# Gate and up of 18 of 22 column pairs by seven products of quarters

## The chip, the cores and the metric

The kernel runs on one core of one Trainium2 chip. The metric is device time in microseconds (us) of one execution; runs of the same program lie within some tenths of a per cent of each other. A core has five engines that work side by side and wait for each other by semaphores: TensorE (PE, matmuls, with its weight loads shown as PEld), VectorE (DVE), ScalarE (ACT), GpSimd (POOL) and SyncE (SP, which here only issues DMA transfers).

## The reference

A decoder trunk of two layers on 512 tokens of width 1024, all in float32. A layer has three attention mixers on one input projection, cross-attention into 256 memory tokens, and a SwiGLU FFN of inner width 2816. What matters here is the FFN:

```
h = rmsnorm(x, norm_ffn[l])
gate_h, up_h = jnp.split(h @ w_gate_up[l], 2, axis=-1)
x = x + (jax.nn.silu(gate_h) * up_h) @ w_down[l]
```

Float32 precision is kept by splitting every operand into a high part (a float32r cast, by ACT) and a low part (the rest, a subtraction on DVE) and by adding three matmuls: high x high, high x low, low x high.

## The kernel before

Activations lie with features on the 128 partitions and the 512 tokens along the row, in eight tiles of 128 features. A weight unit is 128 output columns for all 1024 inputs: a tile of 128 x 1024. `proj` takes one unit: `mm3` (L230) issues 3 matmuls of 512 tokens for each of 8 blocks, 24 in all, into one of three PSUM banks `mm`.

Units are used in a fixed order, the plan. `unit` and `ahead` (L175, L194) load three units on (`load`, SP, three buffers `wraw`) and split one unit on (`halve`: cast `wh` on ACT at L222, subtraction `wl` on DVE at L163; two buffers each). In the FFN the whole `wl` is DVE's (`vcols` is 8).

`skew` (L67) staggers tasks: a task's work after its matmuls is issued behind the matmuls of the next task. Tile, the layer beneath, may then move an instruction on its engine where its operands allow it.

`ffn` (L1190) has 22 pairs of units, gate j and up j. `gate` multiplies its result by 1/rms (`rstd`) as it leaves PSUM and applies Silu; `up` does the same multiplication, multiplies by the gate and splits the product into `h`. The rows of h fall into three parts of 8, 8 and 6; after each part eight `down` tasks add h @ w_down to x. In the last layer the third part's down runs in two halves of 256 tokens (`down_half`, L1238), with the weights kept in `kh` and `kl`. The operand of gate and up is x times the gain, split in `xh` and `xl` before the rms is known, which is why 1/rms is applied afterwards.

## Time and profile before

| what | value |
|---|---|
| median of 3 runs | 2079.9 us (2078.93 to 2082.0) |
| the profiled execution: time, span in the profile | 2081.03 us, 2079.3 us |
| PE, DVE, ACT, POOL busy | 2025.2, 1235.1, 1087.0, 346.4 us |
| Silu of the gates, first layer | 681.8 to 1002.9 us of the span |
| Silu of the gates, second layer | 1705.0 to 2027.1 us |

A time on a row of the profile is an instruction's own duration. Instructions of one engine overlap at their ends, above all matmuls, so that the distance from start to start is what each one costs its engine. "[2.40 <-PE mm L239]" says that the engine was idle for 2.40 us before this instruction and what ended it. The granted clock of TensorE is 1.00 at its upper level of 2.4 GHz and 0.50 at 1.2 GHz.

### The profile page before, as it was taken

How to read it: one execution, taken by the hardware profiler on the slowest of the kernel's cores; microseconds unless marked ns; L12 is line 12 of the kernel's file. 1: busy time of each engine (PE TensorE's matmuls, PEld its weight loads, DVE VectorE, ACT ScalarE, POOL GpSimd, SP SyncE). 2: the span in 40 equal slices, each digit the busy share in tenths (PEclk: the TensorE clock that was granted, in tenths of full speed). 3: DMA queues.
4: the chain of work that ended last, by engine and by line, in shares of the span. 5: the costliest groups of instructions: out<-in, count | busy, mean ns of one | idle time of the engine just before them, and what ended most of it. 6: DMA issues, size and time to landing. Idle time of an engine off the chain costs nothing. (4 is left out here: it accounts for less than half of the span.)

```text
span 2079.3 us, 27775 instructions
## 1 busy us (share of the span) xinstructions
PE 2025.2 (97%) x10072; PEld 1658.0 (80%) x10072; DVE 1235.1 (59%) x2462; ACT 1087.0 (52%) x2196; POOL 346.4 (17%) x302
## 2 busy tenths in 40 slices
PE   7999999999999999999999999999999999999998
PEld 5878887878887788888877788878788878888887
DVE  7786777665457443434567867676655664444354
ACT  5676786884456322222456767777744652222232
POOL 4332122222212000000133212232122010000000
PEclk9999999999999999999999999999999999999999
DMA  6321212233332222322343122132333323233331
GB/s 188 103 73 57 67 46 87 79 105 105 109 102 74 89 92 92 101 91 92 127 123 106 57 67 66 54 88 73 109 117 95 108 68 95 91 92 93 99 107 56
DMA packets 66145, 189.49 MB, mean 91 GB/s; under 512 B 10056, under 2 KB 15944, under 8 KB 66008
## 3 DMA queue, kind: packets, MB, share of 16 engines
q1 hardware_dynamic: 66008, 187.72, 29.3%
q8 instruction: 79, 1.29, 0.3%
q14 instruction: 58, 0.48, 0.1%
HBM read 171.92 MB, written 4.75 MB: 85 GB/s over the span
## 5 line engine op out<-in xcount | busy, mean ns | idle before, releaser
L222 ACT CAST wh<-wraw 128x1024 fp32r<-128x1024 f32 (+3 forms) x311 | 315.4, 1014 | 643.9 <-PE mm L238 364.4
L237 PE MATMUL mm<-xh,wh 128*128 128x512 f32 x1504 | 612.2, 407 | 7.7 <-ACT wh L222 6.3
L238 PE MATMUL mm<-xl,wh 128*128 128x512 f32 x1504 | 602.2, 401 | 2.6 <-DVE xl L173 2.6
L239 PE MATMUL mm<-xh,wl 128*128 128x512 f32 x1504 | 602.6, 401 | 2.0 <-DVE wl L163 1.7
L163 DVE TENSOR_TENSOR wl<-wraw,wh 128x1024 fp32r<-128x1024 f32 (+6 forms) x311 | 339.0, 1090 | 71.6 <-ACT wh L222 65.0
L239 PEld LDWEIGHTS mm<-xh,wl 128*128 128x128 f32 x1504 | 285.5, 190 | 69.1 <-DVE wl L163 3.7
L237 PEld LDWEIGHTS mm<-xh,wh 128*128 128x128 f32 x1504 | 285.9, 190 | 68.0 <-ACT wh L222 6.3
L238 PEld LDWEIGHTS mm<-xl,wh 128*128 128x128 f32 x1504 | 285.9, 190 | 65.5 <-DVE xl L173 5.5
L163 DVE TENSOR_TENSOR tmp<-mm,rstd 128x512 f32<-128x512 f32 (+1 forms) x138 | 90.9, 659 | 275.4 <-PE mm L239 255.6
L163 POOL TENSOR_TENSOR wl<-wraw,wh 128x512 fp32r<-128x512 f32 (+4 forms) x112 | 161.6, 1444 | 518.4 <-ACT wh L222 416.0
L518 ACT ACTIVATE p<-p,st 128x256 f32<-128x256 f32 (+5 forms) x288 | 155.3, 539 | 42.8 <-DVE st L512 38.7
L163 POOL TENSOR_TENSOR acc<-acc,tmp 128x512 f32<-128x512 f32 (+1 forms) x55 | 74.2, 1349 | 599.6 <-ACT tmp L265 438.4
L163 DVE TENSOR_TENSOR x<-x,mm 128x512 f32<-128x512 f32 (+1 forms) x88 | 55.6, 638 | 182.0 <-PE mm L239 182.0
L170 DVE TENSOR_TENSOR pl<-tp,ph 128x256 fp32r<-128x256 f32 (+3 forms) x288 | 131.1, 457 | 50.1 <-ACT ph L169 48.7
L530 ACT ACTIVATE p<-p,st 128x256 f32<-128x256 f32 (+3 forms) x288 | 142.4, 532 | 28.9 <-DVE st L163 17.5
L169 ACT CAST ph<-tp 128x256 fp32r<-128x256 f32 (+3 forms) x288 | 113.1, 395 | 41.1 <-PE tp L448 38.7
L448 PE MATMUL tp<-ident,p 128*128 128x128 f32 x656 | 122.3, 278 | 9.6 <-DVE pl L170 3.6
L512 DVE CUSTOM_DVE_ANT_0 p<-s,causal 128x128 f32<-128x128 f32 (+2 forms) x224 | 106.4, 477 | 41.0 <-PE s L917 16.7
L238 PE MATMUL mm<-h,wh 128*128 128x512 f32 x304 | 120.2, 396 | 0.0
L239 PE MATMUL mm<-h,wl 128*128 128x512 f32 x304 | 120.2, 396 | 0.0
L237 PE MATMUL mm<-h,wh 128*128 128x512 f32 x304 | 120.1, 395 | 0.0
L448 PEld LDWEIGHTS tp<-ident,p 128*128 128x128 f32 x656 | 78.4, 140 | 31.5 <-DVE pl L170 8.7
(242 smaller groups left out, 3297.9 us busy)
## 6 DMA issues: line engine op xcount, KB each, us to landing
wraw<-in_w_in SPq DMA_DIRECT2D x91, 512.0 KB, 3.6
wraw<-in_w_gu SPq DMA_DIRECT2D x88, 512.0 KB, 3.5
wraw<-in_w_d SPq DMA_DIRECT2D x32, 512.0 KB, 3.4
wraw<-in_w_br SPq DMA_DIRECT2D x24, 512.0 KB, 3.6
wraw<-in_w_xkv SPq DMA_DIRECT2D x16, 512.0 KB, 3.4
wraw<-in_w_out SPq DMA_DIRECT2D x16, 512.0 KB, 3.5
wraw<-in_w_d SPq DMA_DIRECT2D x16, 384.0 KB, 3.2
wraw<-in_w_xq SPq DMA_DIRECT2D x8, 512.0 KB, 3.4
```

What stands on the lines that cost most here:

```text
L163: (eng or self.nc.vector).tensor_tensor(out=out, in0=a, in1=b, op=op)
L169: nc.scalar.copy(hi, src)
L170: (eng or nc.vector).tensor_tensor(out=lo, in0=src, in1=hi.bitcast(F32), op=OP.subtract)
L222: nc.scalar.copy(wh[:, j:j + n], raw[:, j:j + n])
L237: nc.tensor.matmul(ps, wh[:, c], xh, start=i == 0, stop=False)
L238: nc.tensor.matmul(ps, wh[:, c], xl, start=False, stop=False)
L239: nc.tensor.matmul(ps, wl[:, c], xh, start=False, stop=i == len(blocks) - 1)
L448: self.nc.tensor.transpose(tp[:, j], src[:, j * 128:j * 128 + 128], self.ident)
L512: o.nc.vector.tensor_tensor_reduce(out=p, in0=self.ps.pop(i), in1=self.mask(self.blocks[i]), scale=-self.scale, scalar=self.init, op0=OP.a ...
L518: self.o.nc.scalar.activation(p, p, AF.Exp, scale=-1.0, bias=st[:, 0, i:i + 1], accum_out=st[:, 1, i:i + 1])
L530: nc.scalar.activation(self.p[j], self.p[j], AF.Copy, scale=self.st[:, 2, j:j + 1])
```

## The change

Four pairs of each layer (j = 0 to 3) stay as they were, apart from a sign. For the other 18 the four quarters of a pair's weights (gate and up, first and second half of the 1024 inputs) and the four quarters of the operand (halves of the inputs, halves of the tokens) are multiplied in the Strassen-Winograd way: seven products p1 to p7 of 128 x 512 by 512 x 256. Each product is `quads`: four blocks of three matmuls of 256 tokens.

- Weight sums: unit `S31` holds gate + up of the first input half and up first + up second half; unit `S24` two further sums built on it; `A22` is the second half of up. Sums and low parts are made on DVE, casts on ACT. The raw up weights have a tile of their own, `up`, with two buffers, read by the sums of S31 and last by the low part of A22 (`dl`). S24 and A22 have one buffer, S31 two.
- Operand: `normed` multiplies x by gain and 1/rms, `sums` makes four differences T (two on GpSimd, two on DVE) and splits them, `operand` writes the split normalised x over the old `xh`, `xl` while the last plain `up` runs through its blocks.
- Results: p1, p6, p7 and p4 of a pair are added up in one PSUM bank (A), and what stands there is copied out in between (s1, s2 by ACT, U by DVE); p5 and p3 share a second bank (D); p2 has a third. Gate halves go to G, up halves to U, with the negative sign that `down` takes off.
- Order: p1(j), p7(j-1), p5(j), p2(j), p4(j-1), p6(j), p3(j), so that a pair's last two products stand among the next pair's. The eight `down` of a part come after p3 of pairs 8 and 16.

```diff
+SUMS, AHEAD, PLAIN = ("S31", "S24", "A22"), 5, 4
...
-        self.load(i + 3)
+        self.load(self.reach(i))
         self.halve(i)
...
+    def reach(self, i):
+
+        plain, j = 0, i
+        while j + 1 < len(self.plan) and j < i + AHEAD and plain < 3:
+            j += 1
+            plain += self.plan[j][0][0] not in SUMS
+        return j
...
     def ahead(self):
         if self.plan is not None:
-            self.load(self.used + 3)
-            self.halve(self.used)
+            i = self.used
+            self.load(self.reach(i))
+            near = [u[0][0] for u in self.plan[i:i + 3]]
+            self.halve(i + 2 if any(t in SUMS for t in near) else i)
...
+            if src[0] in SUMS:
+                self.raw[self.loaded] = self.load_sum(*src)
+                self.loaded += 1
+                continue
...
+            if self.plan[i][0][0] in SUMS:
+                self.ready[i] = self.halve_sum(raw, *self.plan[i][0])
+                self.halved += 1
+                continue
+            if self.plan[i][0][0] == "w_gu":
+                self.gate_raw = raw
...
+    def load_sum(self, kind, l, j):
+
+        if kind != "S31":
+            return None
+        up = self.ups[j] = self.ff.tile([128, 1024], F32, name="up", tag="up", bufs=2)
+        self.nc.sync.dma_start(up, self.a["w_gu"][l, 2 * j + 1])
+        return up
+
+    def halve_sum(self, raw, kind, l, j):
+
+        nc, ff, gate = self.nc, self.ff, self.gate_raw
+        if kind == "A22":
+            h, lo = (ff.tile([128, 512], F32R, name="d" + t, tag="d" + t, bufs=1) for t in "hl")
+            self.split(h, lo, self.ups.pop(j)[:, 512:])
+            return h, lo
+        k = 2 if kind == "S31" else 1
+        s = ff.tile([128, 1024], F32, name="sum", tag=kind + "r", bufs=k)
+        h, lo = (ff.tile([128, 1024], F32R, name=kind + t, tag=kind + t, bufs=k) for t in "hl")
+        if kind == "S31":
+            self.tt(s[:, :512], gate[:, :512], raw[:, :512], OP.add)
+            self.tt(s[:, 512:], raw[:, :512], raw[:, 512:], OP.add)
+            self.sum_raw = s
+        else:
+            self.tt(s[:, :512], self.sum_raw[:, 512:], gate[:, :512], OP.add)
+            self.tt(s[:, 512:], s[:, :512], gate[:, 512:], OP.add)
+        self.split(h, lo, s)
+        return h, lo
...
+    def quads(self, ps, w, off, x, start=True, ahead=False):
+
+        nc = self.nc
+        wh, wl = w
+        for i, (xh, xl) in enumerate(x):
+            c = slice(off + i * 128, off + i * 128 + 128)
+            for k, (a, b) in enumerate(((wh, xh), (wh, xl), (wl, xh))):
+                nc.tensor.matmul(ps, a[:, c], b, start=start and i + k == 0, stop=i == 3 and k == 2,
+                                 skip_group_check=not start)
+            if ahead and i == 0:
+                self.ahead()
+            yield 354
...
+        def up(j):
+            w = self.unit("w_gu", l, 2 * j + 1)
+            ps = self.mm()
+            for i, c in enumerate(self.mm3(ps, w, range(KT), x, ahead=1)):
+                yield c
+                if j == PLAIN - 1 and i % 4 == 3:
+                    operand(range(i - 3, i + 1))
...
+        def normed(kk):
...
+            y = ff.tile([128, 2, 512], F32, name="y", tag="h", bufs=9)
+            for j in range(2):
+                k = 2 * kk + j
+                c = l * G_LAYER + G_FFN + k
+                nc.vector.scalar_tensor_tensor(y[:, j], xt[k], self.gains[:, c:c + 1], n["r"], op0=OP.mult, op1=OP.mult)
+            ys[kk] = y
+
+        def sums(i):
+
+            if i == 0:
+                ts.extend([[ff.tile([128, 4, 256], F32R, name="T", tag="T", bufs=8) for _ in "hl"] for _ in range(4)])
+            c, f = slice(2 * i, 2 * i + 2), [self.tmp((128, 2, 256)) for _ in range(4)]
+            b11, b12, b21, b22 = (ys[k][:, :, h] for k in (i, 2 + i) for h in (slice(0, 256), slice(256, 512)))
+            self.tt(f[0], b11, b12, OP.subtract, nc.gpsimd)
+            self.tt(f[2], b22, b12, OP.subtract, nc.gpsimd)
+            nc.vector.scalar_tensor_tensor(f[1], f[0], -1.0, b22, op0=OP.mult, op1=OP.subtract)
+            nc.vector.scalar_tensor_tensor(f[3], f[1], -1.0, b21, op0=OP.mult, op1=OP.subtract)
+            for t, src in zip(ts, f):
+                self.split(t[0][:, c], t[1][:, c], src)
+
+        def operand(ks):
+
+            for k in ks:
+                c = slice(0, 256 if k < 4 else 512)
+                self.split(x[k][0][:, c], x[k][1][:, c], ys[k // 2][:, k % 2, c])
...
+        def gated(s, c, ps, other):
+            g = s.get("G")
+            if g is None:
+                s["G"] = self.tmp()
+            self.tt(s["G"][:, c], ps, other, OP.add)
+            if g is not None:
+                nc.scalar.activation(g, g, AF.Silu)
+
+        def p1(j):
+            s = pairs[j] = {"A": bank("s", 2)}
+            s["w"] = self.unit("w_gu", l, 2 * j)
+            yield from self.quads(s["A"], s["w"], 0, part_of(0, 0), ahead=True)
+            yield STAGE
+            s["s1"] = kept(s["A"], "s1")
+
+        def p2(j):
+            s = pairs[j]
+            ps = bank("av", 1)
+            yield from self.quads(ps, s["w"], 512, part_of(1, 0))
+            yield STAGE
+            gated(s, slice(0, 256), ps, s["s1"])
+
+        def p5(j):
+            s = pairs[j]
+            s["w31"] = self.unit("S31", l, j)
+            s["D"] = bank("tp", 2)
+            yield from self.quads(s["D"], s["w31"], 512, trans(0), ahead=True)
+            yield STAGE
+            s["s5"] = kept(s["D"], "s5")
+
+        def p6(j):
+            s = pairs[j]
+            s["w24"] = self.unit("S24", l, j)
+            yield from self.quads(s["A"], s["w24"], 0, trans(1), False, ahead=True)
+            yield STAGE
+            s["s2"] = kept(s["A"], "s2")
+
+        def p3(j):
+            s = pairs[j]
+            yield from self.quads(s["D"], s["w24"], 512, part_of(1, 1), False)
+            yield STAGE
+            gated(s, slice(256, 512), s["D"], s["s2"])
+
+        def p7(j):
+            s = pairs[j]
+            yield from self.quads(s["A"], s["w31"], 0, trans(2), False)
+            yield STAGE
+            s["U"] = self.tmp()
+            self.tt(s["U"][:, 256:], s["A"], s["s5"], OP.add)
+
+        def p4(j):
+            s = pairs[j]
+            w = self.unit("A22", l, j, nblk=4)
+            yield from self.quads(s["A"], w, 0, trans(3), False, ahead=True)
+            yield STAGE
+            u, g = s["U"], s["G"]
+            self.tt(u[:, 256:], u[:, 256:], g[:, 256:], OP.mult)
+            self.tt(u[:, :256], s["A"], g[:, :256], OP.mult)
+            o = ff.tile([128, 2, 512], F32R, name="h", tag="h", bufs=9)
+            self.split(o[:, 0], o[:, 1], u)
+            hs[min(j // 8, 2)].append((o[:, 0], o[:, 1]))
+            del pairs[j]
+
+        def after(task, *calls):
+            yield from task
+            for f, i in calls:
+                f(i)
...
-            self.tt(xt[i], xt[i], ps, OP.add)
+            self.tt(xt[i], xt[i], ps, OP.subtract)
...
+        m = sum(FFN_PARTS) - 1
+        tasks = [self.norm_end(st, D, n), gate(0), up(0), after(gate(1), (normed, 0), (normed, 2)),
+                 after(up(1), (normed, 1), (normed, 3)), after(gate(2), (sums, 0)), after(up(2), (sums, 1))]
+        tasks += [gate(3), up(3)]
+        for j in range(PLAIN, m):
+            old = [p7(j - 1), p4(j - 1)] if j > PLAIN else [None, None]
+            new = [p1(j), old[0], p5(j), p2(j), old[1], p6(j), p3(j)]
+            tasks += [t for t in new if t is not None]
+            if j in (8, 16):
+                tasks += [down(i, j // 8 - 1) for i in range(KT)]
+        tasks += [p1(m), p7(m - 1), p5(m), p6(m), p4(m - 1), p3(m), p7(m), p2(m), p4(m)]
```

Not shown: the tiles that hold the last layer's kept weights, the final outputs and the accumulators of the norm take over buffers of the new tiles, `down_half` subtracts too, and four short helpers pick slices.

In the rows below a name's number tells its buffer use; "waits" names the engines or DMA queues whose semaphores an instruction waits for.

First VectorE in the middle of the first layer's FFN, two projections of the kernel before: the gate's and up's results come from bank `mm`, each with the next unit's low part.

```order
L163 TENSOR_TENSOR tmp_8166<-mm_8101,rstd_7062 128x512 [waits PE_49]
L163 TENSOR_TENSOR tmp_8166<-tmp_8166,tmp_8132 128x512 [waits DVE_49,Activation_49]
L163 TENSOR_TENSOR wl_8145<-wraw_8037,wh_8144 128x1024 [waits DMAHW0_49,Activation_49]
L170 TENSOR_TENSOR h_8169<-tmp_8166,h_8169 128x512 [waits Activation_49]
L163 TENSOR_TENSOR tmp_8203<-mm_8135,rstd_7062 128x512 [waits PE_49]
L163 TENSOR_TENSOR wl_8182<-wraw_8071,wh_8181 128x1024 [waits DMAHW1_49,Activation_49]
```

The same place now, one steady pair but for its last two instructions (G's right half, `tp + s2`, and the low part of S24): sums of S31 and S24 (`sum`), U (`s + s5`), G's left half (`av + s1`), low parts `S31l`, `wl`, `dl`.

```order
L166 TENSOR_TENSOR sum_8470<-wraw_8338,up_8361 128x512 [waits DMAHW0_49]
L166 TENSOR_TENSOR sum_8470<-up_8361 128x512
L166 TENSOR_TENSOR tmp_8448<-s_8266,s5_8333 128x256 [waits PE_49]
L166 TENSOR_TENSOR sum_8529<-sum_8470,wraw_8338 128x512 [waits DVE_49]
L166 TENSOR_TENSOR tmp_8448<-tmp_8448,tmp_8356 128x256 [waits DVE_49,Activation_49]
L173 TENSOR_TENSOR S31l_8472<-sum_8470,S31h_8471 128x1024 [waits Activation_49]
L166 TENSOR_TENSOR sum_8529<-sum_8529,wraw_8338 128x512 [waits DVE_49]
L166 TENSOR_TENSOR tmp_8486<-av_8450,s1_8429 128x256 [waits PE_49]
L166 TENSOR_TENSOR wl_8566<-wraw_8468,wh_8565 128x1024 [waits DMAHW6_49,Activation_49]
L173 TENSOR_TENSOR dl_8494<-up_8241,dh_8493 128x512 [waits PE_49,Activation_49]
L166 TENSOR_TENSOR tmp_8448<-s_8266,tmp_8356 128x256
L173 TENSOR_TENSOR h_8508<-tmp_8448,h_8508 128x512 [waits Activation_49]
```

What moved: two results and two low parts per pair became fourteen instructions. The last read of bank `s` (`tmp_8448<-s_8266`) stands behind `wl` and `dl`, and `h` behind it.

SyncE's loads in the first layer's FFN, before:

```order
L205 DMA wraw_7284<-in_w_gu 128x1024 [waits DMAHW7_49,DVE_49]
L205 DMA wraw_7318<-in_w_gu 128x1024 [waits DMAHW0_49,DVE_49]
L205 DMA wraw_7355<-in_w_gu 128x1024 [waits DMAHW1_49,DVE_49]
L205 DMA wraw_7389<-in_w_gu 128x1024 [waits DMAHW2_49,DVE_49]
L205 DMA wraw_7426<-in_w_gu 128x1024 [waits DMAHW3_49,DVE_49]
```

And now, in the steady part (gate units go to `wraw`, up units to `up`):

```order
L222 DMA wraw_8728<-in_w_gu 128x1024 [waits DMAHW5_49,DVE_49]
L260 DMA up_8491<-in_w_gu 128x1024 [waits DVE_49]
L222 DMA wraw_8858<-in_w_gu 128x1024 [waits DMAHW6_49,DVE_49]
L260 DMA up_8621<-in_w_gu 128x1024 [waits DMAHW0_49,DVE_49]
L222 DMA wraw_8988<-in_w_gu 128x1024 [waits DMAHW7_49,DVE_49]
L260 DMA up_8751<-in_w_gu 128x1024 [waits DMAHW2_49,DVE_49]
```

What moved: gate and up loads still alternate, but each kind has its own buffers, and an up load waits for DVE's last read of the up tile before the last.

VectorE at the first pair of seven products of layer 0, from the last sum of the operand's splits on; in the kernel before this place has the rows of the first excerpt.

```order
L166 TENSOR_TENSOR sum_7349<-sum_7295,wraw_7182 128x512
L173 TENSOR_TENSOR xl0_6857<-y_7169,xh0_6856 128x256 [waits PE_49]
L166 TENSOR_TENSOR sum_7349<-sum_7349,wraw_7182 128x512 [waits DVE_49]
L173 TENSOR_TENSOR xl1_6877<-y_7169,xh1_6876 128x256 [waits PE_49]
L173 TENSOR_TENSOR xl2_6904<-y_7212,xh2_6903 128x256 [waits Activation_49]
L173 TENSOR_TENSOR xl3_6925<-y_7212,xh3_6924 128x256 [waits Activation_49]
L173 TENSOR_TENSOR xl4_6952<-y_7172,xh4_6951 128x512 [waits Activation_49]
L173 TENSOR_TENSOR S24l_7351<-sum_7349,S24h_7350 128x1024 [waits Activation_49]
L173 TENSOR_TENSOR xl5_6973<-y_7172,xh5_6972 128x512 [waits PE_49]
L173 TENSOR_TENSOR xl6_7000<-y_7215,xh6_6999 128x512 [waits PE_49]
L173 TENSOR_TENSOR xl7_7008<-y_7215,xh7_7007 128x512 [waits Activation_49]
L166 TENSOR_TENSOR tmp_7390<-mm_7278,rstd_7062 128x512
```

What moved: the second low part of a weight sum stands between the low parts of x that p1 and p2 read, and the result of the last plain gate (`mm_7278`) comes behind them.

## Rows read from the trace of the kernel before

**Rows 1.** The page, busy time and the clock in 40 slices.
```profile
PE 2025.2 (97%) x10072; PEld 1658.0 (80%) x10072; DVE 1235.1 (59%) x2462; ACT 1087.0 (52%) x2196; POOL 346.4 (17%) x302
...
PEclk9999999999999999999999999999999999999999
```
**Rows 2.** Stretches: start:end, length, busy us (instructions) by engine, clock, DMA share, GB/s.
```profile
100.00:200.00 100.00, 94.28 (x527) 76.05 (x526) 77.47 (x217) 73.25 (x187) 28.87 (x29) 1.00 0.23 69
700.00:800.00 100.00, 100.00 (x429) 80.41 (x428) 40.84 (x48) 25.38 (x31) 0.00 (x0) 1.00 0.30 95
800.00:900.00 100.00, 100.00 (x429) 80.40 (x428) 44.10 (x52) 27.36 (x33) 0.00 (x0) 1.00 0.29 91
...
2032.00:2066.00 34.00, 33.11 (x276) 32.85 (x275) 16.75 (x40) 8.69 (x19) 0.00 (x0) 1.00 0.10 32
```
**Rows 3.** DVE in order of time, one pair: start, duration, engine, line, operation, out<-in.
```profile
833.66 0.69 DVE L163 TENSOR_TENSOR tmp<-mm,rstd 128x512 f32<-128x512 f32 x1 [2.40 <-PE mm L239]
...
839.27 0.69 DVE L163 TENSOR_TENSOR tmp<-mm,rstd 128x512 f32<-128x512 f32 x1 [3.50 <-PE mm L239]
840.07 0.69 DVE L163 TENSOR_TENSOR tmp<-tmp 128x512 f32<-128x512 f32 x1
840.68 1.22 DVE L163 TENSOR_TENSOR wl<-wraw,wh 128x1024 fp32r<-128x1024 f32 x1
841.82 0.68 DVE L170 TENSOR_TENSOR h<-tmp,h 128x512 fp32r<-128x512 f32 x1
844.90 0.69 DVE L163 TENSOR_TENSOR tmp<-mm,rstd 128x512 f32<-128x512 f32 x1 [2.40 <-PE mm L239]
```
**Rows 4.** PE in order of time, first and last of 67 matmuls of `down_half`.
```profile
2059.75 0.28 PE L239 MATMUL mm<-h,kl 128*128 128x256 f32 x1
...
2067.67 0.28 PE L239 MATMUL mm<-h,kl 128*128 128x256 f32 x1
```
**Rows 5.** Groups of ACT, 700 to 1000 us: count, busy, mean ns, idle before.
```profile
L222 ACT CAST wh<-wraw 128x1024 fp32r<-128x1024 f32 x53 | 55.8, 1053 | 208.7 <-PE mm L238 136.1 <-issue 72.7
L1200 ACT ACTIVATE tmp<-tmp 128x512 f32<-128x512 f32 x19 | 11.9, 626 | 0.0
L169 ACT CAST h<-tmp 128x512 fp32r<-128x512 f32 x19 | 11.8, 621 | 12.5 <-DVE tmp L163 12.5
```
**Rows 6.** Groups of the whole span: 256 columns on ACT, a kept weight on DVE.
```profile
L169 ACT CAST xos<-av 128x256 fp32r<-128x256 f32 x16 | 6.0, 374 | 4.6 <-PE av L580 4.6
...
L163 DVE TENSOR_TENSOR kl<-wraw,kh 128x768 fp32r<-128x768 f32 x8 | 7.6, 955 | 3.1 <-ACT kh L222 3.1
```
**Rows 7.** DVE in order of time: 256 columns back to back, and behind a matmul.
```profile
632.55 0.42 DVE L170 TENSOR_TENSOR xos<-av,xos 128x256 fp32r<-128x256 f32 x1
632.89 0.41 DVE L170 TENSOR_TENSOR xv<-tp,xv 128x256 fp32r<-128x256 f32 x1
...
2067.99 0.42 DVE L163 TENSOR_TENSOR x<-x,mm 128x256 f32<-128x256 f32 x1 [0.77 <-PE mm L239]
```
**Rows 8.** SP's issue behind `wl`, and DMA: count, KB, median us to landing.
```profile
841.93 0.33 SPq L205 DMA_DIRECT2D wraw<-in_w_gu  x1
...
wraw<-in_w_gu SPq DMA_DIRECT2D x88, 512.0 KB, 3.5
...
w<-in_nsa_w SPq DMA_DIRECT2D x4, 512.0 KB, 5.2
...
DMA to landing us min/median/max: 2.3/3.5/7.0
```
**Rows 9.** DVE in order of time, before the first FFN.
```profile
652.52 1.41 DVE L173 SCALAR_TENSOR_TENSOR xl<-x,gains,xh 128x512 fp32r<-128x512 f32 x2
...
656.18 3.49 DVE L173 SCALAR_TENSOR_TENSOR xl<-x,gains,xh 128x512 fp32r<-128x512 f32 x2
```
**Rows 10.** POOL in the same stretch.
```profile
656.02 3.10 POOL L163 TENSOR_TENSOR acc<-acc,tmp 128x512 f32<-128x512 f32 x2 [0.93 <-ACT tmp L265]
```

More of the change, by code (lines that the diff above doesn't have):

```diff
@@ L116, in drain @@
         pass
+SUMS, AHEAD, PLAIN = ("S31", "S24", "A22"), 5, 4
+KEEP = [("T", 8)] * 8 + [("S31h", 2)] * 2 + [("S31l", 2)] * 2 + [("S31r", 2)] * 2 + [("S24h", 1), ("S24l", 1)]
 CUTS, W1, POS, SQP = 2, 4, 5, (1, 2, 3, 4)
@@ L213, in halve @@
             raw, n = self.raw.pop(i), self.plan[i][1] * 128
+            if self.plan[i][0][0] in SUMS:
[4 more added lines that the diff above has]
+                self.gate_raw = raw
             if self.plan[i][0] in self.kept:
-                wh, wl = (self.ff.tile([128, n], F32R, name=f"k{t}", tag=f"k{t}", bufs=KT) for t in "hl")
+                k = 2 * self.kept.index(self.plan[i][0])
+                wh, wl = (self.ff.tile([128, 1024], F32R, name="kept", tag=KEEP[k + t][0], bufs=KEEP[k + t][1])
+                          for t in range(2))
             else:
@@ L258, in norm_tile @@
         if st["acc"] is None:
-            sq = st["acc"] = st["pool"].tile([128, n], F32, name="acc", tag="acc", bufs=2 if n == 256 and st["pool"] is not self.sh else 1)
+            tag, bufs = ("acc", 1) if st["pool"] is self.sh else ("s5", 2)
+            sq = st["acc"] = st["pool"].tile([128, n], F32, name="acc", tag=tag, bufs=bufs)
             new = True
@@ L1194, in ffn @@
         gs, hs = {}, [[] for _ in FFN_PARTS]
+        self.ff, self.ups = ff, {}
+        ys, ts, pairs = {}, [], {}
         def gate(j):
@@ L1200, in gate @@
             nc.scalar.activation(g, g, AF.Silu)
-        def up(j, part):
-            ps = yield from self.proj(("w_gu", l, 2 * j + 1), x)
+        def up(j):
[5 more added lines that the diff above has]
+                    operand(range(i - 3, i + 1))
             yield STAGE
             u = self.evac(ps, n["r"])
-            self.tt(u, u, gs.pop(j), OP.mult)
+            nc.vector.scalar_tensor_tensor(u, u, -1.0, gs.pop(j), op0=OP.mult, op1=OP.mult)
@@ L1207, in up @@
             o = ff.tile([128, 2, 512], F32R, name="h", tag="h", bufs=9)
             self.split(o[:, 0], o[:, 1], u)
-            hs[part].append((o[:, 0], o[:, 1]))
+            hs[0].append((o[:, 0], o[:, 1]))
+        def normed(kk):
[5 more added lines that the diff above has]
+            ys[kk] = y
@@ new lines, in operand, with part_of, trans, kept @@
+        def operand(ks):
+            for k in ks:
+                c = slice(0, 256 if k < 4 else 512)
+                self.split(x[k][0][:, c], x[k][1][:, c], ys[k // 2][:, k % 2, c])
+        def part_of(k, h):
+            return [(a[:, h * 256:h * 256 + 256], b[:, h * 256:h * 256 + 256]) for a, b in x[4 * k:4 * k + 4]]
+        def trans(i):
+            return [(ts[i][0][:, b], ts[i][1][:, b]) for b in range(4)]
+        def kept(ps, name):
+            s = ff.tile([128, 256], F32, name=name, tag=name, bufs=2 if name == "s5" else 1)
+            nc.scalar.copy(s, ps)
+            return s
@@ new lines, in bank @@
+        def bank(tag, bufs):
+            return self.ps.tile([128, 512], F32, name=tag, tag=tag, bufs=bufs)[:, :256]
+        def gated(s, c, ps, other):
[11 more added lines that the diff above has]
+            s["s1"] = kept(s["A"], "s1")
@@ L1220, in down @@
                 self.norm_tile(st2, xt[i])
-        tasks, f0 = [self.norm_end(st, D, n)], 0
-        for part, kn in enumerate(FFN_PARTS):
-            new = [t for j in range(f0, f0 + kn) for t in (gate(j), up(j, part))]
-            if part:
-                tasks += new[:1] + [down(i, part - 1) for i in range(KT)] + new[1:]
-            else:
-                tasks += new
-            f0 += kn
+        m = sum(FFN_PARTS) - 1
[9 more added lines that the diff above has]
+        tasks += [p1(m), p7(m - 1), p5(m), p6(m), p4(m - 1), p3(m), p7(m), p2(m), p4(m)]
         if not last:
@@ L1232, in ffn @@
             return st2, n2
-        self.ff, self.kept = ff, [("w_d2", l, i) for i in range(KT)]
+        self.kept = [("w_d2", l, i) for i in range(KT)]
         ws, sh, rh = {}, [self.norm_begin(256, nc.vector, ff) for _ in range(2)], [{}, {}]
@@ L1245, in down_half @@
             yield STAGE
-            self.tt(xt[i][:, c], xt[i][:, c], ps, OP.add)
+            self.tt(xt[i][:, c], xt[i][:, c], ps, OP.subtract)
             if i == 0 and half == 0:
@@ L1253, in final @@
             for i in range(KT):
-                t = ff.tile([128, 256], F32, name="fin", tag="fin", bufs=8)
+                if i % 4 == 0:
+                    f = ff.tile([128, 4, 256], F32, name="fin", tag="up", bufs=2)
+                t = f[:, i % 4]
                 c, g = slice(256 * half, 256 * half + 256), G_FINAL + i
```

## The prediction

> **What bounds the kernel now.** I read the busy times of the page first, then the stretches of the two FFNs, then one pair of projections on VectorE, then the only place with the instruction that the change multiplies. On the page TensorE (PE) is busy 97% of the span at a clock of 9 tenths or more in every slice [rows 1]. In the FFN stretches PE shows no idle time at all, VectorE (DVE) is busy 41 to 44% and ScalarE (ACT) 25 to 27% [rows 2]. So there the time is the number of matmuls times their spacing. The busy durations (0.39 us) overlap and are no spacing; the spacing is read from DVE, which takes the result of one 24-matmul projection at 833.66, of the next at 839.27 and of a third at 844.90 [rows 3]: 11.24 us for two, so 11.24 / 48 = 0.234 us per matmul of 512 columns. The pace of 256 columns is seen where the last down projection runs in halves: one starts at 2059.75, and 66 starts later one at 2067.67 [rows 4], 7.92 / 66 = 0.120 us, with the weight loads under them.
>
> **What goes and what comes on PE.** A pair (gate and up) was 48 matmuls, 11.24 us. It becomes seven products of 4 blocks by 3 matmuls of 256 columns, 84 x 0.120 = 10.08 us. That is 1.16 us per pair, and 36 pairs in two layers give 41.8 us. This is all that the change can bring, and only if nothing else makes PE wait. Bounds on the 0.120: it is taken where DVE and ACT are at most half busy [rows 2], in groups of 18 matmuls instead of 12; at 11.24 / 84 = 0.134 us everything is lost, so 14 ns decide. I take 0.120, since the spacing there holds over three changes of bank.
>
> The Trainium skill, "TensorE: Matmul & The Clock Gate", section "Back-to-back issue gap", gives 262 cycles for 256 columns, 109 ns. By that a pair would take 84 x 0.109 = 9.2 us and the gain would be some 74 us; the rows show 0.120 for the same shape, so the sum stays with the rows.
>
> **DVE in a steady pair.** Per pair DVE now has 14 instructions: three subtractions of 1024 columns (low parts of the gate, of S31 and of S24), six of 512 (four adds of the sums, the low part of A22, that of h) and five of 256 out of PSUM or on the gated halves. Back to back a 512 starts 0.61 us before its follower (840.07 to 840.68), a 1024 1.14 us (840.68 to 841.82) [rows 3], a 256 0.34 us [rows 7]. So 3 x 1.14 + 6 x 0.61 + 5 x 0.34 = 8.8 us of 10.08, 87%, where it was 41%. ACT has 3 x 1.05 + 3 x 0.62 + 3 x 0.37 = 6.1 us [rows 5, 6]. Neither is over the budget, but DVE takes its instructions in order, so I walk one turn in the order that the rows on the change show. Let 0 be the end of the product p3 of the pair before; the seven slots are 1.44 us each; an engine sees a PE result some 0.2 us after the slot (2067.67 plus 0.12 to 2067.99) [rows 4, 7]. ACT casts S24h 0.2 to 1.25; DVE takes S24l 1.3 to 2.4, the two adds of S31 to 3.7, U, the first add of S24 and the product with G to 4.9, S31l to 6.1 (its cast ran beside), the second add of S24 and G's left half to 7.1. The gate's wl waits for a cast that waits for p2 (slot ends at 5.76): 5.96 to 7.0, so wl runs 7.05 to 8.2, dl to 8.9, the last product of p4 to 9.2, h and G's right half to 11.0, which is 0.9 into the next turn, ahead of the next S24l (11.4). It closes at PE's 10.08.
>
> Which waits stand last there? The bank of p1 of the pair after next needs that last product of p4: 9.2 against 10.08, a cover of 0.8 us. Queued behind wl and dl on DVE are just that product and h, and PE waits for the first. All other operands are 1.6 us or more early: U frees the bank of p4 at 4.1 against 5.76, S24l is there at 2.5 against 7.2, S31 and the gate a whole turn early.
>
> **The ring of the up buffers.** There are two buffers for the up weights. The load of the next but one is issued when dl of this pair is done; its landing lets the first add of S31 start; ten DVE instructions on (1.22 + 0.34 + 0.61 + 0.34 + 1.14 + 0.61 + 0.34 + 1.14 + 0.69 = 6.43 us) stands the next dl. SP issues 0.03 us after its releaser (841.90 to 841.93), and a load of 512 KB of these weights lands in 3.5 us [rows 3, 8]. The ring is 6.43 + 3.5 + about 0.1 = 10.03 us: as long as PE's turn. It has no slack to recover in; a late landing is first taken from the 0.8 us of the bank. Its bounds: landings ran from 2.3 to 7.0 us, and large loads that queue beside others took 5.2 [rows 8]. Here the gate's load is issued at about 6.8 of a turn and up's at 8.9, so they hardly overlap, and I take 3.5 and put 0.08 us per pair on scatter: 3 us. SP's queue holds loads only, each waiting for DVE; a late up load holds back the next gate load, which is a turn early.
>
> **The way in.** The normalised operand, the four T sums and their splits must be made in the four plain pairs. DVE gets eight products of 0.69, four T sums of 0.69, eight T splits of 0.61, eight splits of x (4 x 0.34 + 4 x 0.61) and the sums of the first pair (3 x 0.61 + 2 x 1.14): 5.5 + 2.8 + 4.9 + 3.8 + 4.1 = 21.1 us. Beside them stand three plain pairs at 41% of 11.24, 13.9 us. 35.0 us in the 33.7 us of six projections: DVE is the bound for once, by 1.3 us at least. Four subtractions on GpSimd (POOL) run there too, and the trace shows what they do: two VectorE operations take 1.41 us at 652.52 but 3.49 us at 656.18, when POOL adds 512 columns twice beside them [rows 9, 10]. About 1 us each, up to 4 us more; and the second Strassen pair's S31l stands behind the late evacuations of the last plain pair. Ends: 1.3 and 8 us per layer. I take 4.5, the middle, as half of POOL's operations will find a DVE instruction to hold: 9 us in both layers. After the down projections the weights are ready and DVE was idle 60%: nothing. At the end of the last layer h of the last pair needs, after p4, 0.2 + 0.42 + 0.62 + 0.69 = 1.9 us, and two subtractions for kept weights (0.95 each) [rows 6] can stand between, 3.8 us; PE has 15 other matmuls first, 1.8 us: 0 to 2, I take 1 us more than the 0.9 of 34 that are lost there now [rows 2].
>
> **Sum.** Of the profiled execution's 2081.0 us: -41.8 + 3 + 9 + 1 = -28.8, 2052.2 us. It lies 1.1 us above the median of the runs (2079.9), so **2051 us** for the median.
>
> **Rivals.**
> - *The ring sets the pace, still a gain.* If up lands in 4.3 us, 0.8 more than now, a turn is 10.8 us: 36 x 0.75 = 27 us lost, less the 0.8 us of cover in each of six stretches (5): 2073 us. For it: the ring is as long as PE's turn. Against: the DMA engines are 30% busy [rows 2], and the loads alternate.
> - *The ring is longer than the old pair: slower.* From a landing of 11.24 - 6.53 = 4.7 us on there is no gain, and at the 5.2 us that queued loads took a turn is 11.73 us, 0.49 over the old pair: 36 x 0.49 + 10 = +28, 2108 us. For it: 7.0 was seen, and DVE can lengthen its 6.4 us too, if something shares its ports; against: POOL is idle there.
> - *256 columns don't keep 0.120 in groups of 12.* A bubble of 0.1 us at each product would cost 36 x 7 x 0.1 = 25 us: 2076 us. Against: three changes of bank in [rows 4] without one.
> - *The clock falls.* The clock is 1.00, the 2.4 GHz level, even where attention leaves PE 5.7% idle in many small waits (100 to 200 us) [rows 2]; so shorter groups should keep it. If a tenth of the 363 us of Strassen products ran at 1.2 GHz, that would be +36 us, 2087 us. The Trainium skill, same page, section "A second HAM failure mode: psum-queue depth-cycling", describes just this danger, banks changed each turn and PE idle in small bits; the row of attention speaks against it here.
> - *The change doesn't do what it says*: the built program's order has 84 matmuls of 256 columns per pair, so none.
>
> **Chances and range.** PE keeps the pace 0.67 (own range 2041 to 2062: way in 1.3 or 8 us a layer, scatter 0 to 7 us); ring, still a gain 0.16; ring, slower 0.07; bubbles 0.06; clock 0.04. The range 2040 to 2071 takes the first case and most of the second. A measurement of this kernel tells 0.2% (4 us) from nothing. Faster: 0.67 + 0.13 + 0.03 + 0.01 = 0.84; same 0.05; slower 0.11.
>
> **What would show it.** Right: the starts of 256-column matmuls 0.120 us apart in the middle of a layer's FFN; S31l to S31l of the next pair 10.1 us; DVE about 87% busy with no idle time before S31's first add that ends on a DMA; PE idle 2 to 8 us around each layer's first Strassen pair and nearly none after it. Wrong: S31's add waiting for the up load turn after turn and PE waiting for DVE at p1 or p4 (ring); PE spaced wider with no releaser named (bubbles); a granted clock under 1.00 in the stretch.

## The result and the profile after

In the runs made side by side the changed kernel took 2050.1 us (median of 4, 2049.4 to 2052.5), the kernel before 2079.4 us (median of 4): a ratio of 0.986, 95% interval 0.984 to 0.988. Two later series of the same kernel on other occasions gave 2045.9 and 2049.2 us, beside 2080.8 and 2080.5 us of before. So the gain is 29 to 35 us, and a single series is worth some 3 us either way. The forecast was 2051 us.

The page after, to be held against [rows 1]:

```profile
span 2047.7 us, 31024 instructions
...
PE 1986.3 (97%) x11368; PEld 1694.6 (83%) x11368; DVE 1412.9 (69%) x2806; ACT 1194.2 (58%) x2408; POOL 358.5 (18%) x310
```

PE has 1296 instructions more and 39 us less busy time; DVE has 178 us more. The page's line of the granted clock is the one of [rows 1], 9 tenths or more in every slice. The clock is not at its upper level throughout: in both kernels it falls to 0.50 for some us ahead of an FFN and at the end of the span, but in these two it never does so within the FFN stretches. The stretches after, against [rows 2] (length, busy us with instructions of PE, PEld, DVE, ACT, POOL, then clock, DMA share, GB/s):

```profile
700.00:800.00 100.00, 98.17 (x610) 87.37 (x609) 76.67 (x112) 47.34 (x72) 2.98 (x2) 1.00 0.32 100
800.00:900.00 100.00, 97.80 (x745) 93.56 (x744) 73.99 (x114) 48.54 (x75) 0.00 (x0) 1.00 0.33 101
900.00:1000.00 100.00, 100.00 (x648) 90.80 (x647) 63.39 (x93) 39.75 (x58) 0.00 (x0) 1.00 0.28 85
...
2015.00:2036.00 21.00, 21.00 (x177) 20.95 (x176) 10.27 (x26) 5.37 (x12) 0.00 (x0) 1.00 0.15 51
```

Before, PE had no idle time in the first two stretches of an FFN that [rows 2] shows, and 0.9 us of 34 at the end. Now 1.8 us are missing in the first of these stretches, 2.2 in the second and none in the third or at the end. The second stretch lies nearly whole in the middle eight pairs, and one turn of its DVE reads (start, duration, operation, and in brackets the idle time before it with what ended it):

```profile
854.40 0.69 DVE L166 TENSOR_TENSOR sum<-wraw,up 128x512 f32<-128x512 f32 x1 [0.93 <-DMA up<-in_w_gu]
...
858.96 1.22 DVE L166 TENSOR_TENSOR wl<-wraw,wh 128x1024 fp32r<-128x1024 f32 x1
860.09 0.68 DVE L173 TENSOR_TENSOR dl<-up,dh 128x512 fp32r<-128x512 f32 x1
860.69 0.42 DVE L166 TENSOR_TENSOR tmp<-s,tmp 128x256 f32<-128x256 f32 x1
...
865.02 0.69 DVE L166 TENSOR_TENSOR sum<-wraw,up 128x512 f32<-128x512 f32 x1 [1.05 <-DMA up<-in_w_gu]
```

The first add of S31 waits for its up load turn after turn, and a turn is 10.62 us (854.40 to 865.02). `dl` is done at 860.77; SP issues the next up load then; it lands at 865.0. In the SP queue, and in the list of DMA issues of 800 to 900 us (count, KB of one, median us to landing), one sees why the landing is longer than the 3.5 us of [rows 8]:

```profile
858.74 0.33 SPq L222 DMA_DIRECT2D wraw<-in_w_d  x1
860.80 0.33 SPq L260 DMA_DIRECT2D up<-in_w_gu  x1
```

```profile
up<-in_w_gu SPq DMA_DIRECT2D x8, 512.0 KB, 4.1
wraw<-in_w_gu SPq DMA_DIRECT2D x6, 512.0 KB, 3.6
```

Another 512 KB load is issued 2.06 us ahead of each up load, and the second of the two takes 4.1 us. What PE lost is seen in its own rows, at the way in (first three), at p1 of a middle pair and at p4 of the pair ahead of the second downs:

```profile
716.57 0.39 PE L290 MATMUL s<-xl,wh 128*128 128x256 f32 x1 [1.03 <-DVE xl L173]
...
730.48 0.50 PE L290 MATMUL s<-T,S24h 128*128 128x256 f32 x2 [0.49 <-ACT S24h L172]
731.26 0.39 PE L290 MATMUL tp<-xh,S24h 128*128 128x256 f32 x1 [0.29 <-ACT s L1324]
...
861.16 0.39 PE L290 MATMUL s<-xh,wh 128*128 128x256 f32 x1 [0.28 <-DVE tmp L166]
...
889.37 0.50 PE L290 MATMUL s<-T,dh 128*128 128x256 f32 x2 [1.14 <-DVE tmp L166]
```

A start that comes later than the spacing allows is the loss; it is some 0.15 us more than the bracket says. Added up over both layers, the ring of the up buffers cost 5.8 us in this execution (4.8 and 6.4 in the two later ones), the way in 5.0 us.

For all kernels below one yardstick is used beside the median: the time from the first to the last Silu of an FFN, both layers added. It leaves out the part between the FFNs, where single executions differ by some microseconds (why is said further down).

| kernel | median us | FFN stretches, us |
|---|---|---|
| before | 2079.4 to 2080.9 | 643.1 |
| changed (three series) | 2050.1, 2045.9, 2049.2 | 618.0, 617.1, 618.6 |
| up3 | 2041.9 | 611.2 |
| halves | 2042.1 | 612.7 |
| early | 2044.0 | 614.6 |
| add | 2046.1 | 615.1 |
| up3_add | 2046.1 | 615.3 |
| subdve | 2049.6 | 619.8 |
| late | 2053.0 | 625.6 |
| plain3 | 2052.7 | 618.3 |
| best1 | 2037.8 | 607.2 |

(The last Silu stands nearer to the end of its pair after the change: from there to the end of the span it was 52.2 us before and 48.2 after. Against before, 4.0 us a layer must be taken off each figure below the first row, and plain3 has one pair more by products.)

### The profile page after: what moved, and what is told of

Its sections match the earlier page's. It is cut to its first block, busy times and chain, and to the rows that moved or that the text cites. A ratio compares the mean times of both kernels' runs of the same rounds, so it can differ in the third digit from the quotient of the medians.

```text
span 2047.7 us, 31024 instructions
## 1 busy us (share of the span) xinstructions
PE 1986.3 (97%) x11368; PEld 1694.6 (83%) x11368; DVE 1412.9 (69%) x2806; ACT 1194.2 (58%) x2408; POOL 358.5 (18%) x310
## 5 line engine op out<-in xcount | busy, mean ns | idle before, releaser
L247 ACT CAST wh<-wraw 128x1024 fp32r<-128x1024 f32 (+3 forms) x275 | 277.6, 1009 | 385.0 <-PE mm L304 210.9
L303 PE MATMUL mm<-xh,wh 128*128 128x512 f32 x928 | 384.7, 415 | 7.4 <-ACT wh L247 6.1
L304 PE MATMUL mm<-xl,wh 128*128 128x512 f32 x928 | 374.1, 404 | 3.6 <-DVE xl L176 3.6
L305 PE MATMUL mm<-xh,wl 128*128 128x512 f32 x928 | 374.4, 404 | 2.1 <-DVE wl L166 1.9
L166 DVE TENSOR_TENSOR wl<-wraw,wh 128x1024 fp32r<-128x1024 f32 (+5 forms) x275 | 296.1, 1077 | 63.0 <-ACT wh L247 56.5
L305 PEld LDWEIGHTS mm<-xh,wl 128*128 128x128 f32 x928 | 177.2, 191 | 43.0 <-DVE wl L166 3.8
L303 PEld LDWEIGHTS mm<-xh,wh 128*128 128x128 f32 x928 | 177.5, 191 | 41.3 <-ACT wh L247 6.1
L304 PEld LDWEIGHTS mm<-xl,wh 128*128 128x128 f32 x928 | 177.9, 192 | 40.0 <-DVE xl L176 6.5
L303 PE MATMUL mm<-oh,wh 128*128 128x512 f32 x192 | 79.4, 413 | 0.0
```

What stands on the lines that cost most here:

```text
L166: (eng or self.nc.vector).tensor_tensor(out=out, in0=a, in1=b, op=op)
L247: nc.scalar.copy(wh[:, j:j + n], raw[:, j:j + n])
L303: nc.tensor.matmul(ps, wh[:, c], xh, start=i == 0, stop=False)
L304: nc.tensor.matmul(ps, wh[:, c], xl, start=False, stop=False)
L305: nc.tensor.matmul(ps, wl[:, c], xh, start=False, stop=i == len(blocks) - 1)
```

## The experiments

The four of the first group ran together, again, late, best1 and subdve in a second, again2, halves and plain3 in a third. The first group had no run of the changed kernel beside it, so its medians are read against before in the same group (2080.9) and by the FFN stretches. The theory that I held was R: what the middle segments lose is the ring of two up buffers. Its rival was V: VectorE is simply too full.

**up3: a third up buffer.**

```diff
-        up = self.ups[j] = self.ff.tile(..., name="up", tag="up", bufs=2)
+        up = self.ups[j] = self.ff.tile(..., name="up", tag="up", bufs=3)
...
-        s = ff.tile(..., name="sum", tag=kind + "r", bufs=k)
+        s = ff.tile(..., name="sum", tag=kind + "r", bufs=1)
```

(Not shown: the last layer's kept weights and the final outputs follow the new numbers of buffers.)

> A third buffer for the raw weight of `up` (its 4 KB come from the second buffer of the S31 sums, which the profile shows unused). Theory R (the ring of the two up buffers is what the middle eight pairs lose: the gaps of PE that wait for VectorE at the first product's bank sum to 3.8 us over both layers, and one gap of 2.0 us stands at each layer's second group of downs): S31's first add no longer waits for a load, S31l to S31l is 10.1 us in the middle segment, and the time falls by 4 to 6 us to about 2045. Theory V (VectorE itself is too full there: 8.8 us of work in a turn of 10.1, which wins nothing by an earlier load): 2049 to 2051, no change.

Measured: 2041.9 us (2037.7 to 2046.8), FFN stretches 6 to 7 us shorter than the changed kernel's. Five turns, from one S31l to the fifth after it, in the view of stretches, then SP's issues in the same place and the landing:

```profile
825.33:875.33 50.00, 50.00 (x423) 50.00 (x422) 45.23 (x72) 30.13 (x45) 0.00 (x0) 1.00 0.33 106
```

```profile
845.14 0.33 SPq L222 DMA_DIRECT2D wraw<-in_w_gu  x1
850.22 0.33 SPq L260 DMA_DIRECT2D up<-in_w_gu  x1
```

```profile
up<-in_w_gu SPq DMA_DIRECT2D x8, 512.0 KB, 3.5
```

A turn is 10.00 us, PE has no idle time, and the wait of S31's add for the load, 7.7 us in six pieces between 800 and 900 us before, is not there. DVE does the same work, 9.05 us of 10.00. The loads now stand 5 us apart, and up lands in 3.5 us again. V falls: the same work on DVE costs PE nothing. For R this run is not clean, since Tile ordered DVE anew here: the first add of S31 stands behind S31l (846.84 in this turn, with no wait) and no longer ahead of it. That the ring alone does it is shown by `halves` below, where the order is kept.

**add: the first add of S31 twice, two buffers; up3_add: the same with three.**

```diff
             self.tt(s[:, :512], gate[:, :512], raw[:, :512], OP.add)
+            self.tt(s[:, :512], gate[:, :512], raw[:, :512], OP.add)
```

> The first add of every S31 sum is issued twice (0.68 us more on VectorE a pair, the sum is the same), with two up buffers. Theory R: the extra add stands between the landing of up and the release of its buffer, so a turn grows from 10.6 to about 11.3 us wherever the ring sets the pace: some 9 us in each middle segment instead of 2.9, and 2 to 5 us in each of the two shorter segments, 2065 to 2075 in all. Theory V (only VectorE's sum of work counts, 9.5 us of 10.08): 0 to 3 us, 2050 to 2053.

> Third up buffer and the doubled add together. Theory R: without the ring the extra 0.68 us lies within the 1.3 us a pair that VectorE has free: within 2 us of the kernel with three buffers alone, 2045 to 2047, which makes the same add cost 15 us or more with two buffers and under 2 us with three. Theory V: as with two buffers, 0 to 3 us over the changed kernel, 2050 to 2053.

Measured: 2046.1 us both. For `add` R had said 2065 or more, and that was wrong, for a reason that the trace shows:

```profile
856.84 0.69 DVE L166 TENSOR_TENSOR sum<-wraw,up 128x512 f32<-128x512 f32 x1 [0.96 <-DMA up<-in_w_gu]
...
862.12 0.41 DVE L166 TENSOR_TENSOR tmp<-s,tmp 128x256 f32<-128x256 f32 x1
862.45 0.68 DVE L173 TENSOR_TENSOR dl<-up,dh 128x512 fp32r<-128x512 f32 x1
863.05 1.22 DVE L166 TENSOR_TENSOR wl<-wraw,wh 128x1024 fp32r<-128x1024 f32 x1
...
867.14 0.69 DVE L166 TENSOR_TENSOR sum<-wraw,up 128x512 f32<-128x512 f32 x1 [0.80 <-DMA up<-in_w_gu]
```

The additional instruction made Tile order DVE anew: `dl` and p4's last product (`tmp<-s,tmp`) now stand ahead of `wl` and not behind it. So 1.14 us left the ring while the further add and that product (0.60 and 0.33) came in; and the gate's load now stands 2.4 us ahead of up's, which lands in 4.0 us. A turn is 10.30 us (856.84 to 867.14), 0.3 less than in the changed kernel, and p1's bank comes free 5.28 us after S31's first add in place of 6.29. PE no longer waits there. The experiment changed two things at once and says nothing against the ring; it shows how much hangs on the place of one instruction. `up3_add` has another order on DVE than `up3` (the second add of S31 stands behind `dl`), but the same steady turn of 10.00 us with DVE at 96%, so 0.6 us of further work costs nothing there, and the 4.3 us between the two come from the way in, where PE waits 1.55 us at the first product and 1.08 at p2 of the first pair.

```profile
827.37:877.36 49.99, 49.99 (x423) 49.99 (x422) 48.21 (x77) 30.12 (x45) 0.00 (x0) 1.00 0.33 106
```

**halves: the up load in two halves, two buffers, the same order on DVE.**

```diff
-        self.nc.sync.dma_start(up, self.a["w_gu"][l, 2 * j + 1])
+        for c in (slice(0, 512), slice(512, 1024)):
+            self.nc.sync.dma_start(up[:, c], self.a["w_gu"][l, 2 * j + 1][:, c])
```

> Two up buffers, VectorE's order as in the changed kernel; the up weight is loaded in two halves of 256 KB, so that S31's first add needs only the first half. Theory R with the landing as its other part: the second add starts 4.1 us after the issue in place of 4.7, a turn of the ring is 10.0 us in place of 10.6, the gaps at p1 go and the time falls by 4 to 5 us against the reference. Rival L2 (a transfer's landing is mostly fixed time, so the halves land one behind the other and no earlier): turn 10.4 to 10.7, no change.

Measured: 2042.1 us (2039.3 to 2045.8) beside 2049.2 of the reference, 5.9 us off the FFN stretches. Five turns, the landings of the halves (each from its own issue), and SP and DVE in one of the turns:

```profile
825.13:875.12 49.99, 49.99 (x423) 49.99 (x422) 44.76 (x71) 29.39 (x46) 0.00 (x0) 1.00 0.34 106
```

```profile
up<-in_w_gu SPq DMA_DIRECT2D x16, 256.0 KB, 3.6
```

```profile
859.23 0.80 SPq L261 DMA_DIRECT2D up<-in_w_gu  x2
```

```profile
862.73 0.69 DVE L166 TENSOR_TENSOR sum<-wraw,up 128x512 f32<-128x512 f32 x1
```

The first half is there in time for S31's first add, which starts 3.5 us after the first issue (859.23 to 862.73) and has no wait of its own. The whole weight is there no earlier than before: the second add starts at 863.39, 4.16 us after the first issue, as R had said. Half a microsecond less in the ring removes PE's waits at p1 (those at p4 ahead of the second downs shrink to 0.43 and 0.25 us), with DVE's order as in the changed kernel: the ring is confirmed with its two buffers in place, and the remedy takes no memory.

**late: the up load twice, two buffers.**

```diff
-        self.nc.sync.dma_start(up, self.a["w_gu"][l, 2 * j + 1])
+        for _ in range(2):
+            self.nc.sync.dma_start(up, self.a["w_gu"][l, 2 * j + 1])
```

> Two up buffers; every up weight is loaded twice into its buffer, one load behind the other, so that it is there some 7.2 us after the first issue in place of 4.1. Behind this the built program has another order on VectorE: dl stands three instructions behind S31's first add (0.61 + 0.61 + 0.34 + 0.69 = 2.3 us), not nine (6.4 us). Theory R (the ring is the VectorE work from S31's first add to dl, plus the load): 2.3 + 7.2 + 0.1 = 9.6 us, under PE's 10.05, so the gaps at p1 and p4 go although the load is twice as long: 2042 to 2046. Rival L (the time until an up load has landed is what counts, wherever dl stands): 3 us more a turn, 2070 or more.

Measured: 2053.0 us (2051.4 to 2058.8), FFN stretches 8.5 us longer than again's. Neither number was right. VectorE and SP:

```profile
846.54 0.69 DVE L166 TENSOR_TENSOR sum<-wraw,up 128x512 f32<-128x512 f32 x1 [2.20 <-DMA up<-in_w_gu]
...
848.09 0.68 DVE L173 TENSOR_TENSOR dl<-up,dh 128x512 fp32r<-128x512 f32 x1
...
856.89 0.69 DVE L166 TENSOR_TENSOR sum<-wraw,up 128x512 f32<-128x512 f32 x1 [1.02 <-DMA up<-in_w_gu]
```

```profile
848.80 0.33 SPq L261 DMA_DIRECT2D up<-in_w_gu  x1
851.74 0.33 SPq L222 DMA_DIRECT2D wraw<-in_w_gu  x1
852.29 0.33 SPq L261 DMA_DIRECT2D up<-in_w_gu  x1
```

In the view of waits of SP's queue, 830 to 890 us (total, times, longest), the second load waits for the first one each time:

```profile
SPq L261 <- DMA up<-in_w_gu: 6.1, 5, 3.2
```

`dl` is done at 848.8, and the first load is issued there. The second load writes the same buffer and is issued only when the first has landed, 3.49 us later; it lands 4.6 us after its own issue, with the gate's load 0.55 us ahead of it. So the ring is 2.26 us from S31's first add to the first issue, 3.49 and 4.60: 10.35 us, which is the turn (846.54 to 856.89). R's sum was right in its form. Its two loads take 8.1 us and not the 7.2 that I had assumed, so the ring stays above PE's 10.0 and the waits do not go. L's 2070 was wrong too: the second load adds some 4.0 us to the ring, and the early `dl` takes 4.1 away. The largest single loss is one wait at p1 of the third pair by products, 2.63 us, behind which the matmuls of 256 columns stand 0.21 us apart for 3.4 us, at a granted clock of 0.50.

**early: the normalising and the T sums one task earlier, two buffers.**

```diff
-        tasks = [..., gate(0), up(0), after(gate(1), (normed, 0), (normed, 2)),
-                 after(up(1), (normed, 1), (normed, 3)), after(gate(2), (sums, 0)), after(up(2), (sums, 1))]
+        tasks = [..., gate(0), after(up(0), (normed, 0), (normed, 2)), after(gate(1), (normed, 1), (normed, 3)),
+                 after(up(1), (sums, 0)), after(gate(2), (sums, 1)), up(2)]
```

> Two up buffers. The multiplications that make the normalised operand and the T sums are issued one task earlier each (behind the first up instead of the second gate, and so on). Theory W (the gap of 1.19 and 0.98 us before each layer's first Strassen product comes from VectorE's work being bunched late: it idles 8 us at 680 to 697 us and then has no idle from 700 to 730 us): these gaps go, minus 1.5 to 2.5 us, 2047.5 to 2048.5. Rival H (VectorE is held by GpSimd's two subtractions, whose instructions beside it take longer, and these only move along): the T lows still take 0.91 us, the gaps stay within 0.5 us of what they were, 2049.5 to 2050.5, or a new gap stands in the plain pairs.

Measured: 2044.0 us (2041.8 to 2045.6), FFN stretches 2.5 to 4 us shorter. First the changed kernel, then `early`, in the stretches ahead of the first product, with PE at that product behind it:

```profile
690.00:700.00 10.00, 10.00 (x44) 8.06 (x43) 6.98 (x11) 3.27 (x5) 1.29 (x1) 1.00 0.35 107
...
710.00:730.00 20.00, 18.93 (x132) 17.16 (x130) 20.00 (x33) 14.09 (x24) 0.00 (x0) 1.00 0.15 48
```

```profile
690.00:700.00 10.00, 10.00 (x44) 8.06 (x43) 10.00 (x16) 5.05 (x8) 2.59 (x2) 1.00 0.35 107
```

```profile
716.12 0.38 PE L290 MATMUL s<-xl,wh 128*128 128x256 f32 x1
...
729.88 0.51 PE L290 MATMUL s<-T,dh 128*128 128x256 f32 x2 [0.54 <-DVE tmp L166]
```

VectorE idled 3 us of the ten before 700 and was full from there on. With the work brought forward it is full from 690 on, and the loss of the way in falls from 2.4 to 0.9 us a layer. W holds. GpSimd's hold, H's part, is still there (T's low parts take up to 1.19 us), but the gaps do not move along with it. The time fell by more than the 1.5 to 2.5 us that W had said.

**subdve: the T subtractions on VectorE in place of GpSimd.**

```diff
-            self.tt(f[0], b11, b12, OP.subtract, nc.gpsimd)
-            self.tt(f[2], b22, b12, OP.subtract, nc.gpsimd)
+            self.tt(f[0], b11, b12, OP.subtract)
+            self.tt(f[2], b22, b12, OP.subtract)
```

> Two up buffers; the four T subtractions of a layer that GpSimd made are made by VectorE. Theory H (GpSimd's operations hold VectorE instructions beside them, which is why the T low parts take 0.91 us each in place of 0.61 and why VectorE is late at the first product): T lows fall to 0.61 to 0.70, the gap of 1.0 to 1.2 us before each layer's first product shrinks or stays, since 4 x 0.61 = 2.4 us come back as VectorE's own work: 2048 to 2050. Rival (GpSimd's work is free beside VectorE): VectorE is 2.4 us later per layer, the gap grows to some 3.5 us, 2053 to 2056.

Measured: 2049.6 us beside 2045.9 of again, FFN stretches 2.7 us longer. In the changed kernel GpSimd and VectorE stand side by side so:

```profile
703.20 1.68 POOL L166 TENSOR_TENSOR tmp<-y 128x512 f32<-128x512 f32 x1 [11.55 <-DVE T L173]
705.51 1.30 POOL L166 TENSOR_TENSOR tmp<-y 128x512 f32<-128x512 f32 x1 [0.63 <-DVE T L173]
```

```profile
703.64 1.78 DVE L173 TENSOR_TENSOR T<-tmp,T 128x512 fp32r<-128x512 f32 x1
705.35 0.68 DVE L166 TENSOR_TENSOR tmp<-mm,rstd 128x512 f32<-128x512 f32 x1
705.96 1.40 DVE L173 TENSOR_TENSOR T<-tmp,T 128x512 fp32r<-128x512 f32 x1
```

Two of the low parts took 1.78 and 1.40 us; on VectorE alone all take 0.68. So GpSimd's four subtractions cost VectorE 1.8 us, and VectorE's own four cost 2.4: H is right in its mechanism. That GpSimd is still the better place by a little fits both sums, but 2.7 us is near the edge of what can be told here (the three executions of the changed kernel spread over 1.5 us in this yardstick). The Trainium skill, "SBUF — State Buffer", section "Who interferes with whom", says that a VectorE instruction with two inputs in SBUF and a GpSimd instruction that reads SBUF exclude each other, and that order decides who waits. These rows agree, down to the evacuation between the two (0.68 us), whose one input is in PSUM.

**best1: up3 and early together; plain3: best1 with three plain pairs.**

```diff
-SUMS, AHEAD, PLAIN = ("S31", "S24", "A22"), 5, 4
+SUMS, AHEAD, PLAIN = ("S31", "S24", "A22"), 5, 3
...
-        tasks += [gate(3), up(3)]
```

> Third up buffer and the normalising one task earlier, together. If the two losses are apart (ring 5.8 us, way in 2 x 1.6 us), the time is that of the changed kernel minus 8 to 10 us, 2039 to 2042, and PE shows no gap in the middle segments and 0.9 us a layer at the first Strassen pair. If earlier normalising only works with a late VectorE elsewhere, no better than with the third buffer alone.

> As best1 (third buffer, normalising early), with a nineteenth pair of each layer made by seven products: three plain pairs in place of four. Pace alone says two pairs x 1.24 = 2.5 us less than best1, 2035. Theory W (VectorE bounds the way in: in best1 it has no idle time from 690 to 738 us): a plain pair took 11.2 us of TensorE and 4.6 us of VectorE, so 6.6 us of cover go with it and come back as PE's waits before and in the first Strassen pairs: 2 x (6.6 - 1.2) = 11 us slower than best1, 2046 to 2050.

Measured: best1 2037.8 us (2034.1 to 2040.0), 0.979 of before (0.978 to 0.980) and 8 us under the changed kernel of the same series; the two losses are apart. It is the fastest version of this study. plain3 took 2052.7 us, and its FFN stretches are 11.1 us longer than those of best1, as W's sum said, though not quite by its mechanism; the median lies above W's 2046 to 2050. GpSimd, PE and the stretches around the first products of plain3:

```profile
699.93 11.87 POOL L166 TENSOR_TENSOR tmp<-y 128x512 f32<-128x512 f32 x2 [8.54 <-issue]
```

```profile
712.09 0.39 PE L290 MATMUL tp<-T,S31h 128*128 128x256 f32 x1 [2.10 <-ACT T L172]
713.54 0.38 PE L290 MATMUL s<-xh,wl 128*128 128x256 f32 x1 [1.07 <-DVE wl L166]
```

```profile
710.00:714.00 4.00, 0.85 (x4) 0.65 (x5) 3.43 (x4) 3.17 (x5) 1.80 (x2) 1.00 0.01 2
714.00:716.00 2.00, 2.00 (x15) 2.00 (x14) 2.00 (x5) 0.62 (x1) 0.00 (x0) 0.71 0.00 0
716.00:718.00 2.00, 2.00 (x11) 2.00 (x11) 2.00 (x4) 0.75 (x2) 0.00 (x0) 0.50 0.00 0
```

With VectorE nearly full (11.3 of these 11.9 us), GpSimd's two subtractions take 11.9 us in place of 3, so that T comes late, PE idles 3 of 4 us, and behind that the granted clock falls to its lower level, 0.50, for the next products. A part of the 11 us is this clock: by the last two rows some 1.6 us in this layer, an estimate from 0.29 of 2 us and half of 2 us.

**again, again2: the changed kernel as it is**, the references used above.

> The changed kernel once more, on the chip and in the rounds of the three others, since a difference of 2 to 8 us has to be read on one chip: 2048 to 2052.

> The changed kernel a third time, as the reference for the two beside it: 2045 to 2051, the spread of the two earlier series.

## Why the prediction came out as it did

The median was forecast to 1 us, but that is partly luck: three terms were off by 3 to 4 us, in both directions.

- *PE's pace: right, a little small.* Forecast -41.8 us by 0.120 us a matmul. Without other waits (up3, halves) 84 matmuls take 10.00 us, 0.119 each, so 1.24 us a pair and -44.6 us. Groups of 12 keep the pace of groups of 18, and within the FFN stretches the clock stays up: the rivals of bubbles and of the clock did not come. The 109 ns by the Trainium skill, "TensorE: Matmul & The Clock Gate", section "Back-to-back issue gap", did not come either; that page gives them for a matmul by itself.
- *VectorE in a steady pair: right.* 8.8 us forecast, 9.05 measured, and no cost of its own: with 9.6 us (up3_add) PE still does not wait.
- *The ring of the up buffers: right in its parts, wrong in one.* The VectorE part, 6.43 us, measured 6.37 (854.40 to 860.77). The step that failed is "so they hardly overlap": the gate's load 2.1 us ahead, as forecast, makes up land in 4.1 us, not 3.5. By the forecast's own numbers the two loads, 2.1 us apart and 3.5 us long, overlap by 1.4 us. The turn was 10.6 us, not 10.03, and 5 to 6 us were lost, not 3. S31's add waits for the up load turn after turn, the sign that the forecast had named for the ring. This is the first rival (the ring sets the pace, still a gain), but only in the middle segments: in the first the early turns of VectorE are 7.6 to 8.7 us long (S31l to S31l), since its loads lie ready, and in the last they are 10.8, 10.1 and 10.0; in neither does PE come to wait. That is why it cost 6 us and not 27. The wait at p4 ahead of the second downs (1.30 and 0.74 us) was not in the forecast: there S31's sum for the pair behind the downs waits for its load and U stands behind it on VectorE.
- *The way in: right in kind, too large.* Forecast 9 us, measured 5.0. VectorE is the bound there, as `early` shows. GpSimd held it for 1.8 us a layer, inside the 1 to 4 that I allowed; but the loss that I added for the second pair's S31l was 0.2 us.
- *Down restart and end:* nothing at the restart, as forecast. At the end 1 us more was forecast; instead the 0.9 us that PE lost there before are gone (33.11 of 34.00 us busy in [rows 2], 21.00 of 21.00 now).

Measured terms: -44.6 + 5.8 + 5.0 - 0.9 = -34.7 us. The stretches show less: 643.1 to 618.0 and 2 x 4.0 at the pairs' ends make -33.1. Of the 1.6 us between the two, 1.0 can be placed at the ring, since the stretches of up3, which has none of its waits, are 6.8 us shorter and not 5.8; the rest is open.

The span fell by 31.6 us in the two profiled executions, 1.5 less than the FFNs. The record shows why: the part between the FFNs (last Silu of the first layer to first Silu of the second, less the 4.0 us) took 1.7 us more, and the clock there differs between executions. Ahead of the second FFN PE waits 1.67 us for DVE's `xl` at the norm in both of two executions, and some 2 us later the clock of 6 us reads so, in the changed kernel and then in `again`, which is the same program:

```profile
1682.00:1688.00 6.00, 6.00 (x16) 4.53 (x15) 1.30 (x3) 0.73 (x2) 0.00 (x0) 0.57 0.27 87
```

```profile
1682.00:1688.00 6.00, 6.00 (x25) 4.52 (x24) 2.31 (x4) 3.13 (x5) 0.00 (x0) 1.00 0.30 87
```

The same part took 699.9 us in the first and 697.0 in the second. Over 20 us at this place the granted clock was 0.91 in the kernel before (1690 to 1710 us) and 0.83 in the changed one (1675 to 1695 us), which is 1.8 and 3.4 us lost: the difference is 1.6 of the 1.7 us. So some of the 3 us by which single executions and series differ is this clock, and not the change.

## What to carry to other kernels

A ring through a buffer is the work between its first read and its release, plus the load, which takes longer the nearer another load stands ahead of it (and plus a second load, where that waits for the first). Here it was 10.6 us against a pace of 10.0, so half a microsecond in any part decided, and a third buffer or a load in two halves bought it off. An experiment that adds an instruction or a buffer under a scheduler has to be read by its order first. Where a change fills an idle engine, its price is at the entry, where preparation and the last old work meet, and bringing the preparation forward cost nothing here.
